# A diffusion layer with 32 experts on one core: one size of weight slot for all experts, and another order of the routing chain

## The chip, the cores and the metric

The program runs on one core of a Trainium2 chip. The metric is the device time of one execution in microseconds (us). The kernel before was run three times: 2148.13 to 2154.74 us, median 2150.1 us. The profile is of one further execution.

## The reference

One layer over 1024 tokens of width 1024. The first part mixes tokens (a state-space branch and a pooling branch, merged by gates, one output projection). A post-norm follows, and then a mixture of 32 experts in 4 groups of 8. Cut to what the change touches, with `hf` the normed and modulated tokens:

```
lg  = hf @ w_rg + b_rg                       # 4 group scores; the best group is taken
le  = (hf @ w_re + b_re)[best group]         # 8 expert scores; the best two are taken
w   = p_group * softmax(top two scores)
y   = sum over the two: w * ((silu(x @ Wg[e]) * (x @ Wu[e])) @ Wd[e])
out = layer_norm(alpha * x_mid + gate * y)
```

Wg and Wu of an expert are 1024x512, Wd is 512x1024, all float32: 6 MiB for each expert, 192 MiB in all. How many tokens an expert gets is known only when the last token has been routed.

## The kernel before, in words

The mixing takes the first 1440 us or so. Then eight tiles of 128 tokens go through the output projection, the norm and the router (the loop over `t`). In each, `choose(t)` picks group and experts on VectorE; `place(t)` finds each token's rank among the tokens of the three *fixed* experts 29, 30, 31 (32 rows each) by two matmuls with a triangular and an all-ones matrix, and adds it to `pidf`, the list of tokens of these 96 rows. `place` runs five tiles late (`LAG`), so that after the last tile five of them are left. The normed tokens `hx` go to DRAM (`h2_d`, shown as `h_d`); a gather fetches rows of it by the list `xfix` (fixed experts) or by a column of `xidx` (the others) into a tile `xe`.

After the last tile comes the dispatch chain, nearly all on VectorE: count tokens for each expert, rank the other 29 experts by load, give the fullest one 256 rows (one expert, called D here), four 192 (E), eight 128 (S), twelve 64 (two of them in one block, P) and four 32 (in one block, Q), place all tokens, and make `xidx`; `tab` is the list of experts in order of rank, from which SyncE takes the addresses of their weights. The blocks run as: fixed, D, E, Q, E, E, S, P, E, and so on. In a block, TensorE transposes gathered rows (`L1394`), multiplies by gate and up (`mm`), ScalarE and VectorE make silu and product (`eh`), TensorE transposes that and multiplies by down (`py`); the result is scattered to DRAM. Blocks of one expert (D, E, S) split weights into a rounded part and a rest (`sh` on ScalarE L1372, `sl` on VectorE L1373). Blocks of several experts (fixed, Q, P) multiply in float32, each expert with its own columns of the array, at L1411.

Weights come through a ring of 16 slots of 8 KB in each partition (`wa`, `wb`), loaded in order by SyncE (`load_w`, L1227); a slot's next load waits until its last reader is done. In `load_w` a slot holds `ne` experts with `4 // ne` steps of 128 rows each: one expert fills a slot by one DMA of 1 MiB (8 KB runs), two by two of 512 KB (4 KB runs), four by four of 256 KB (2 KB runs), and the fixed three use 6 KB of a slot by three of 256 KB. So the fixed experts' weights take 24 loads of a slot, Q's and each P's likewise 24 and 12, a single's 6. Before the end of routing, 14 slots of the fixed experts are loaded ahead (12 of their 18 MiB with the two that GpSimd issues after the first gather); SyncE then waits, in its order, for slots that TensorE must first finish reading.

Of the kernel before, what the change touches and what calls it, by code (L numbers as in the profile page):

```python
# [103 lines left out]
LAG = 5  # L104
# [37 lines left out]
def _emit(tc, nc, es, ins, out, dbg, stop):  # L142
# [815 lines left out]
    gp = rg.enter_context(pool("gp", side="right"))  # L958
    r0g = row(gp, ins["ln"][0], "r0g")
    r0b = row(gp, ins["ln"][1], "r0b")  # L960
    lgt = gp.tile([P, NT, 36], F32, name="lgt")
    G2 = row(gp, mod_d[0, 2 * D:3 * D], "G2")
    B2 = row(gp, mod_d[0, D:2 * D], "B2")
# [21 lines left out]
    ohhf = gp.tile([P, NT, 2, 4], F32R, name="ohhf")  # L985
# [8 lines left out]
    def choose(t):  # L994
# [28 lines left out]
        A = gp.tile([P, NE], F32, name="A", bufs=LAG + 1)  # L1023
# [5 lines left out]

    def place(t, A):  # L1030
        def tl(shape, name):
            return gp.tile([P] + shape, F32, name=name, bufs=2)

        T.matmul(pos[:, t], cst[:, C_SPRE], A, start=True, stop=False)
        T.matmul(pos[:, t], ones, bsum[:, t], start=False, stop=True)


        pf = pos[:, t, NE - NF:]
        okf = tl([NF], "okf")
        V.tensor_scalar(okf, pf, float(FIX_CAP), None, op0=OP.is_lt)  # L1040
        pb = tl([NF], "pb")
        V.tensor_tensor(pb, pf, ct[:, 341:341 + NF], op=OP.add)
        of = tl([2, NF], "of")
        V.tensor_tensor(of, o12[:, :, t, NE - NF:], b1_(okf, 2), op=OP.mult)
        lp = tl([2, 2, NF], "lp")
        V.tensor_tensor(lp[:, 0], of, b1_(pb, 2), op=OP.mult)
        V.tensor_tensor(lp[:, 1], of, b2(aid.rearrange("p (k t) -> p k t", k=2)[:, :, t], NF), op=OP.mult)
        lv = tl([2, 2], "lv")
        V.tensor_reduce(lv, lp, axis=AX.X, op=OP.add)
        lo = lv[:, 0]  # L1050
        V.tensor_copy(ohhf[:, t, :, 0], lv[:, 1])
        ohlf = gp.tile([P, 2, P], F32R, name="ohlf", bufs=1)
        last = V.tensor_tensor(ohlf, b1_(iop, 2), b2(lo, P), op=OP.is_equal)
        for k in range(2):
            T.matmul(pidf, ohlf[:, k], ohhf[:, t, k], start=(t + k == 0), stop=(t == NT - 1 and k == 1))
        return last

    def weights():
        S.activation(ge, ge, AF.Exp)
        pg = kept.tile([P, NT], F32, name="pg")  # L1060
        V.tensor_reduce(pg, ge, axis=AX.X, op=OP.add)
        V.reciprocal(pg, pg)
        V.tensor_sub(v12[:, 1], v12[:, 1], v12[:, 0])
# [4 lines left out]
        V.tensor_tensor(wk[:, 1], wk[:, 0], v12[:, 1], op=OP.mult)  # L1068

    with pool("o_sb") as op_:  # L1070
# [10 lines left out]
        bT2 = gp.tile([P, 4, P], F32, name="bT2")  # L1081
# [60 lines left out]
        for t in range(NT):  # L1142
# [12 lines left out]
            for n in range(2):  # L1155
                if t >= LAG and n == 0:
                    place(t - LAG, As[t - LAG])
                if t >= 2 and n == 1:
                    wout(*a, 1)
                turn(r, hT, n)  # L1160
# [18 lines left out]
            G.dma_start(h2_d[t * P:(t + 1) * P], hx)  # L1179
# [30 lines left out]
    def load_w(evs):  # L1210

        ne = len(evs)
        kc = PER // ne
        res = []
        for i0 in range(0, NSTEP, kc):
            w = wslot([ne, kc, 512])
            f = slice(i0 % PER * 512, (i0 % PER + kc) * 512)
            for i, ev in enumerate(evs):
                if isinstance(ev, int):
                    src = ins["w_e"][ev, i0 // PER, :, f]  # L1220
                else:
                    src = ins["w_e"][bass.ds(ev, 1), i0 // PER, :, f].rearrange("a p f -> p (a f)")
                dst = w[:, i].rearrange("p k f -> p (k f)")
                if ns[0] - 1 in N_GA:
                    late.append((dst, src))
                else:
                    Q.dma_start(dst, src)  # L1227
            res.append(w)
        return res, kc

    late = []
# [3 lines left out]
    gathered = []  # L1235
    loads = []

    def gather(xi):
        xe = xes[nblk[0] % NXE]
        if nblk[0] < NXE:  # L1240
            with tc.issue_after(loads[1].ins) if nblk[0] > 1 else ExitStack():
                G.memset(xe, 0.0)
        nblk[0] += 1
        ga = G.indirect_dma_start(out=xe, out_offset=None, in_=h2_d[:, :],  # L1244
                                  in_offset=bass.IndirectOffsetOnAxis(ap=xi, axis=0), bounds_check=L - 1,
                                  oob_is_err=False)
        loads.append(ga)
        return xe


    with pool("gq", side="right") as gq:
# [3 lines left out]
        def rows_of(pid, n, name, x, y=None):  # L1255

            fi = tl([n], name + "f")
            V.tensor_scalar(fi, pid, 0.0, 8192.0, op0=OP.is_equal, op1=OP.mult)
            V.tensor_tensor(fi, fi, pid, op=OP.add)
            gi = tl([n], name + "g")  # L1260
            V.tensor_scalar(gi, fi, float(L + 1), -float(L), op0=OP.is_ge, op1=OP.mult)
            V.scalar_tensor_tensor(x, gi, -1.0, fi, op0=OP.add, op1=OP.add)
            if y is not None:
                V.tensor_scalar(y, fi, -1.0, None, op0=OP.add)

        rows_of(pidf[:, 0:1], 1, "fx", xfix)
        gathered.append(gather(xfix))
        for w, src in late:
            with tc.issue_after(loads[-1].ins):
                G.dma_start(w, src)  # L1270

        e32 = slice(0, NE)
        fixed, ecol = ct[e32, 337:338], ct[e32, 340:341]
        pc = bank("st")
        cr = pc[:, 0:NE]
        cc = pc[e32, NE:NE + 1]
        T.matmul(cr, ones, bsum[:, NT], start=True, stop=True)
        T.matmul(cc, bsum[:, NT], ones[:, 0:1], start=True, stop=True)
        kr = tl([NE], "kr", NE)
        kc = tl([1], "kc", NE)  # L1280
        V.scalar_tensor_tensor(kr, cr[e32], 32.0, ct[e32, 40:72], op0=OP.mult, op1=OP.add)
        V.scalar_tensor_tensor(kc, cc, 32.0, ct[e32, 336:337], op0=OP.mult, op1=OP.add)
        V.tensor_scalar(kr, kr, kc, None, op0=OP.is_gt)
        rk = tl([1], "rk", NE)
        V.tensor_reduce(rk, kr, axis=AX.X, op=OP.add)
        V.scalar_tensor_tensor(rk, fixed, 64.0, rk, op0=OP.mult, op1=OP.add)

        ns_ = len(STEPS)
        cb2 = tl([2, ns_], "cb2", NE)
        V.tensor_scalar(cb2[:, 0], ct[e32, 144:144 + ns_], rk, None, op0=OP.is_gt)  # L1290
        V.tensor_scalar(cb2[:, 1], ct[e32, 144:144 + ns_], rk, None, op0=OP.min)
        V.tensor_tensor(cb2, cb2, ct[e32, 152:152 + 2 * ns_].rearrange("p (a n) -> p a n", a=2), op=OP.mult)
        cols = tl([3], "cols", NE)
        V.tensor_reduce(cols[:, 0:2], cb2, axis=AX.X, op=OP.add)
        V.tensor_tensor(cols[:, 0:2], cols[:, 0:2], ct[e32, 338:340], op=OP.add)
        cap = cols[:, 0:1]

        rem = tl([1], "rem", NE)
        V.tensor_tensor(rem, cc, cap, op=OP.subtract)
        nbx = tl([8], "nbx", NE)  # L1300
        V.tensor_scalar(nbx, ct[e32, 72:80], rem, None, op0=OP.is_lt)
        nb = tl([1], "nb", NE)
        V.tensor_reduce(nb, nbx, axis=AX.X, op=OP.add)
        po = pc[e32, 64:65]
        T.matmul(po, cst[e32, C_SPRE, 0:NE], nb, start=True, stop=True)
        ovs = tl([1], "ovs", NE)
        V.tensor_copy(ovs, po)
        V.tensor_scalar(cols[:, 2:3], ovs, 128.0, float(NSTAT), op0=OP.mult, op1=OP.add)
        V.tensor_tensor(cols[:, 2:3], cols[:, 2:3], cap, op=OP.subtract)
        V.tensor_tensor(cols[:, 1:2], cols[:, 1:2], cols[:, 2:3], op=OP.subtract)  # L1310
# [3 lines left out]
        T.matmul(rows, ones[e32], dg, start=True, stop=True)  # L1314
# [20 lines left out]
        for h in range(2):  # L1335
# [3 lines left out]
            for j0 in (8 * h, 8 * h + 4):  # L1339
                ohl = gq.tile([P, 4, P], F32R, name="ohl", bufs=3)  # L1340
# [305 lines left out]
```

## Time and profile before

| | us |
|---|---|
| median of three runs | 2150.1 |
| profiled execution | 2157.08 |
| its span, first to last instruction | 2155.3 |
| TensorE busy in it | 2001.2 |
| VectorE busy | 1393.1 |
| ScalarE busy | 895.3 |
| mean granted TensorE clock | 0.971 |

All rows are of one core. PE is TensorE's multiplications, PEld its loads of the stationary operand, DVE VectorE, ACT ScalarE, POOL GpSimd, SP SyncE. In a row "[0.42 <-DMA wb]" is the idle time of the engine before it and what ended that. L1343 is line 1343 of the kernel before.

### The profile page before, as it was taken

To read this page: it belongs to the slowest core of one execution; us is meant where nothing else is said; L and a number is where in the kernel's file an instruction comes from. 1 tells how busy PE (TensorE), PEld (TensorE's weight loads), DVE (VectorE), ACT (ScalarE), POOL (GpSimd) and SP (SyncE) were. 2 spreads that over 40 slices of the span, in tenths; PEclk is the share of its full clock that TensorE was granted. 3 is DMA by queue.
4 is the path that set the end of the run, shared out by engine and by line. 5 is a ranking of instruction groups with operands and counts; after the bars stand their busy time and mean duration, and the time that the engine had idled before them with its cause. 6 is when DMAs were issued, how large, how long until landed. Compare 5 with 4: busy or idle time off the path is not lost. (4 is left out here: it accounts for less than half of the span.)

```text
span 2155.3 us, 28781 instructions
## 1 busy us (share of the span) xinstructions
PE 2001.2 (93%) x10086; PEld 1521.6 (71%) x10086; DVE 1393.1 (65%) x2281; ACT 895.3 (42%) x1589; POOL 453.4 (21%) x435
## 2 busy tenths in 40 slices
PE   6998999999999999999999998989699899999985
PEld 3787788887888888888878787777365576554452
DVE  4554467779668887877665765687553576543377
ACT  3422254455454655655342331221143465533362
POOL 3233211112122222321101111253310021200003
PEclk9999999999999999999999999999699999999997
DMA  7122234333443332443477666526699999999966
GB/s 302 59 96 78 96 100 111 113 99 104 120 129 98 108 114 82 148 137 97 158 266 229 222 223 190 186 92 212 228 384 342 405 394 386 380 413 410 407 247 239
DMA packets 171902, 441.93 MB, mean 205 GB/s; under 512 B 19997, under 2 KB 54045, under 8 KB 160745
## 3 DMA queue, kind: packets, MB, share of 16 engines
q1 hardware_dynamic: 154282, 399.67, 52.8%
q0 software_dynamic: 9984, 26.75, 3.2%
q10 hardware_dynamic: 7488, 13.63, 1.7%
q8 instruction: 80, 1.31, 0.3%
q14 instruction: 68, 0.56, 0.1%
HBM read 403.01 MB, written 46.28 MB: 208 GB/s over the span
## 5 line engine op out<-in xcount | busy, mean ns | idle before, releaser
L186 PE MATMUL mm<-hh,whi 128*128 128x512 f32 x1024 | 415.1, 405 | 0.0
L188 PE MATMUL mm<-hh,wlo 128*128 128x512 f32 x1024 | 401.4, 392 | 4.2 <-DVE wlo L183 4.2
L187 PE MATMUL mm<-hl,whi 128*128 128x512 f32 x1024 | 401.1, 392 | 0.0
L188 PEld LDWEIGHTS mm<-hh,wlo 128*128 128x128 f32 x1024 | 192.9, 188 | 46.1 <-DVE wlo L183 4.6
L186 PEld LDWEIGHTS mm<-hh,whi 128*128 128x128 f32 x1024 | 193.1, 189 | 38.4 <-issue 2.6
L187 PEld LDWEIGHTS mm<-hl,whi 128*128 128x128 f32 x1024 | 193.5, 189 | 35.6 <-issue 0.2
L1372 ACT ACTIVATE sh<-wb 128x512 fp32r<-128x512 f32 x280 | 169.7, 628 | 96.0 <-DMA wb<-in_w_e_dram 22.6
L704 ACT ACTIVATE rb<-rb,tmx 128x128 f32<-128x128 f32 x512 | 163.2, 390 | 106.5 <-POOL rb L697 105.0
L1373 DVE TENSOR_TENSOR sl<-wb,sh 128x512 fp32r<-128x512 f32 x280 | 180.4, 685 | 38.9 <-ACT sh L1372 32.9
L183 DVE TENSOR_TENSOR wlo<-wraw,whi 128x1024 fp32r<-128x1024 f32 x65 | 81.7, 1257 | 161.7 <-ACT whi L182 151.4
L697 POOL TENSOR_SCALAR_AFFINE_SELECT rb<-rb 128x512 f32<-128x512 f32 x128 | 110.5, 869 | 301.9 <-DMA rb<-sr_d 229.8
L186 PE MATMUL mm<-zh,bhi 128*128 128x512 f32 x384 | 154.0, 401 | 2.2 <-ACT bhi L182 2.2
L188 PE MATMUL mm<-zh,blo 128*128 128x512 f32 x384 | 152.5, 397 | 0.4 <-DVE blo L183 0.4
L187 PE MATMUL mm<-zl,bhi 128*128 128x512 f32 x384 | 152.3, 397 | 0.0
L182 ACT ACTIVATE whi<-wraw 128x1024 fp32r<-128x1024 f32 x65 | 68.5, 1053 | 129.3 <-PE mm L187 86.4
L182 ACT ACTIVATE bhi<-braw 128x1024 fp32r<-128x1024 f32 x48 | 50.8, 1059 | 142.0 <-PE mm L187 124.5
L1411 PE MATMUL mm<-wb,xh 128*64 128x512 f32 (+1 forms) x516 | 108.9, 603 | 0.3 <-ACT xh L1400 0.3
L518 DVE SCALAR_TENSOR_TENSOR xT<-craw,sm,xT 128x1284 f32<-128x1284 f32 x64 | 101.4, 1585 | 3.1 <-ACT xT L516 2.8
L1244 POOL DMA_INDIRECT xe<-h_d,xidx x25 | 27.3, 1091 | 333.9 <-PE tr L1394 304.5
L187 PE MATMUL mm<-sl,xh 128*128 128x512 f32 x224 | 88.7, 396 | 5.1 <-DVE sl L1373 5.1
L183 DVE TENSOR_TENSOR blo<-braw,bhi 128x1024 fp32r<-128x1024 f32 x48 | 65.7, 1369 | 39.4 <-ACT bhi L182 36.9
L186 PE MATMUL mm<-sh,xh 128*128 128x512 f32 x224 | 89.0, 397 | 2.1 <-ACT sh L1372 2.1
(470 smaller groups left out, 4054.8 us busy)
## 6 DMA issues: line engine op xcount, KB each, us to landing
wb<-in_w_e_dram SPq DMA_DIRECT2D x70, 1024.0 KB
wb<-in_w_e_dram SPq DMA_DIRECT2D x120, 512.0 KB
wb<-in_w_e_dram SPq DMA_DIRECT2D x142, 256.0 KB
wraw<-in_w_blk_dram SPq DMA_DIRECT2D x64, 512.0 KB
rb<-sr_d SPq DMA_DIRECT2D x128, 256.0 KB
F<-sr_d SPq DMA_DIRECT2D x64, 256.0 KB
wmr<-in_w_ada_dram SPq DMA_DIRECT2D x64, 256.0 KB
braw<-in_wa_blk_dram SPq DMA_DIRECT2D x32, 512.0 KB
```

Source lines behind the costliest of these rows:

```text
L182: S.activation(hi, src, AF.Copy)
L183: V.tensor_sub(lo, src, hi.bitcast(F32))
L186: T.matmul(ps, lh, rh, start=start, stop=False, **kw)
L187: T.matmul(ps, lh, rl, start=False, stop=False, **kw)
L188: return T.matmul(ps, ll, rh, start=False, stop=stop, **kw)
L518: V.scalar_tensor_tensor(o, raw[:, j:j + n], smc(SM_CW + b * KCONV + j), o, op0=OP.mult, op1=OP.add)
L697: G.affine_select(rv, rv, pattern=[[0, 2], [0, 2], [sg, P]], base=0, channel_multiplier=-sg, compare_op=OP.is_ge, fill=NEG_BIG)
L704: S.activation(e, e, AF.Exp, bias=tmx[:, 0, 2 * n + ih, hd:hd + 1])
L1244: ga = G.indirect_dma_start(out=xe, out_offset=None, in_=h2_d[:, :], in_offset=bass.IndirectOffsetOnAxis(ap=xi, axis=0), bounds_check=L - ...
L1372: S.activation(hi, w, AF.Copy)
L1373: V.tensor_tensor(lo, w, hi.bitcast(F32), op=OP.subtract)
L1411: T.matmul(pss[0][i * W:(i + 1) * W], ls[0][0][:, k, i * W:(i + 1) * W], wt[:, i], start=(k == 0), stop=(k == nk - 1))
```

## The change

- Every load of expert weights becomes one DMA of 1 MiB into a slot of its own (4 steps of one expert); the products of several experts read several slots. The fixed experts take 18 loads instead of 24.
- `place` handles pairs of tiles by one set of VectorE instructions, earlier (`PLACE_AT`); three tiles, in two calls, are left after the last one.
- The last tile's `hx` is made on VectorE by two instructions of high priority from `r` before its norm, instead of on GpSimd. The two instructions on `r` with r0g, r0b come after `tab` instead of after `place`.
- The fixed rows have a tile of their own (`xe_fix`) and are gathered right when `xfix` is there; unused rows take token 0 instead of being left as a cleared tile, so that the memsets of gathered tiles go away (those of the first blocks likewise).
- `ranks` (counting, ranking, `tab`) is issued before the fixed products; the fixed gate and up products are issued before the matmuls that place all tokens (`pid`).
- The lists for the first four gathered tiles are clamped to 0, `value_load`s stand behind the loads of the block before, and the one-hot tiles `ohl` have two buffers instead of three.

The core of the diff:

```
-        ne = len(evs)
-        kc = PER // ne
-        for i0 in range(0, NSTEP, kc):
-            w = wslot([ne, kc, 512])
-            f = slice(i0 % PER * 512, (i0 % PER + kc) * 512)
-            for i, ev in enumerate(evs):
+        for i0 in range(NSTEP // PER):
+            for ev in evs:
+                w = wslot([PER, 512])
...
+    def exact_product(ps, xh, w, s0, nk, ne, W):
+        for k in range(nk):
+            wt = [a[:, (s0 + k) % PER] for a in w[(s0 + k) // PER]]
+            for i in range(ne):
+                last = T.matmul(ps[i * W:(i + 1) * W], xh[:, k, i * W:(i + 1) * W], wt[i], start=(k == 0),
+                                stop=(k == nk - 1))
+            if s0 + k in (3, 2 * KD - 1):
+                marks.append(last)
...
-LAG = 5
+PLACE_AT = {5: (0, 2), 6: (2, 4), 7: (4, 5), 8: (5, 7)}
...
+            if t == NT - 1:
+                with tc.high_priority(offset=HP):
+                    V.scalar_tensor_tensor(hx, r, ag[:, 0:1], G2, op0=OP.subtract, op1=OP.mult)
+                    V.scalar_tensor_tensor(hx, hx, rs, B2, op0=OP.mult, op1=OP.add)
...
+                place(*PLACE_AT[NT])
+                place(PLACE_AT[NT][1], NT)
+                xe_fix = op_.tile([P, D], F32, name="xe_fix", tag="wor", bufs=2)
+                pc, cols, tabbed = ranks(xe_fix)
...
-            E = G if t == NT - 1 else V
-            E.tensor_tensor(hx, r, G2, op=OP.mult)
-            E.tensor_tensor(hx, hx, B2, op=OP.add)
...
-            with tc.issue_after(fence.ins) if t == NT - 1 else ExitStack():
+            with tc.issue_after(tabbed.ins) if t == NT - 1 else ExitStack():
                 E.tensor_tensor(r, r, r0g, op=OP.mult)
                 E.tensor_tensor(r, r, r0b, op=OP.add)
...
-            with tc.issue_after(loads[1].ins) if nblk[0] > 1 else ExitStack():
-                G.memset(xe, 0.0)
...
+        for m in range(2):
+            ps = bank("mm")
+            exact_product(ps, xh, fixed_w, m * KD, KD, NF, FIX_CAP)
+            begun.append([ps])
...
+        with tc.issue_after(marks[0].ins):
+            T.matmul(rows, ones[e32], dg, start=True, stop=True)
...
+                with tc.issue_after(marks[1].ins):
+                    for j in range(4):
+                        T.matmul(pid, ohl[:, j], ohh[:, j0 + j], start=(j0 + j == 0), stop=(j0 + j == 2 * NT - 1))
...
-    weights()
-    block([(xfix, yidx[:, 0:1], False)], fixed_w, len(FIXED), FIX_CAP)
+    weights(placed)
+    block([(xfix, yidx[:, 0:1], False)], fixed_w, len(FIXED), FIX_CAP, begun)
```

The order of instructions is the same on TensorE up to the last tiles of the routing. There, TensorE's order before had the fixed products (L1411) behind the matmuls that place all tokens (L1343):

```order
L1278 MATMUL st<-cst,bsum 32x1
L1055 MATMUL mm<-ohhf,ohlf 128x4 x4
L1305 MATMUL st<-nb,cst 32x1
L1314 MATMUL st<-dg,cst 128x96
L1394 MATMUL st<-cst,xe_12416 128x128 x4
L1394 MATMUL tr<-cst,xe_12416 128x128 x4
L1343 MATMUL py<-ohh,ohl 128x50 x4
L1352 MATMUL py<-oh,rct 1x64
L1353 MATMUL py<-nb,cst 1x1
L1343 MATMUL py<-ohh,ohl 128x50 x12
L1411 MATMUL mm<-wa_12360,xh 32x512 x3
```

Now the fixed rows' transposes (L1343) and products (L1324) come first. The placing matmuls (now L1384) stand at the end of gate and up, and D's first gathered tile (`xe_12396`) is transposed ahead of the fixed experts' down product:

```order
L1324 MATMUL mm<-wb_12386,xh 32x512
L1324 MATMUL mm<-wb_12388,xh 32x512
L1324 MATMUL mm<-wb_12390,xh 32x512
L1384 MATMUL py<-ohh,ohl 128x50 x16
L1481 MATMUL tr<-cst,eh 128x96 x4
L1435 MATMUL st<-cst,xe_12396 128x128 x3
L1324 MATMUL py<-wb_12392,ehh 32x512
```

In the order before, the first transposes of D's rows stood among the fixed experts' up product.

GpSimd before, from the last tile on (`hx` and its two arithmetic instructions, then memsets, gathers and the six late loads):

```order
L1177 TENSOR_TENSOR hx<-r,G_11100 128x1024
L1178 TENSOR_TENSOR hx<-hx,B_11102 128x1024
L1179 DMA h_d<-hx 128x1024
L1184 DMA r_d<-r 128x1024
L1242 MEMSET xe_12416 128x1024
L1242 MEMSET xe_12417 128x1024
L1244 DMA xe_12416<-h_d,xfix 128x1024
L1270 DMA wb_12420<-in_w_e_dram 128x512 x3
L1270 DMA wb_12421<-in_w_e_dram 128x512 x3
L1244 DMA xe_12417<-h_d,xidx 128x1024
```

GpSimd now, over the same stretch:

```order
L1259 DMA h_d<-hx 128x1024
L1082 DMA xe_fix<-h_d,xfix 128x1024
L1269 DMA r_d<-r 128x1024
L1337 DMA wb_12400<-in_w_e_dram 128x2048
L1337 DMA wb_12401<-in_w_e_dram 128x2048
L1082 DMA xe_12396<-h_d,xidx 128x1024
L1082 DMA xe_12397<-h_d,xidx 128x1024
```

GpSimd has no arithmetic left there, and the late loads are two of 1 MiB instead of six of 256 KB.

## Rows read from the trace of the kernel before

**Rows 1.** Stretches of the span: busy us and instructions of each engine
```profile
core 0: us, PE busy (x) PEld busy (x) DVE busy (x) ACT busy (x) POOL busy (x), PEclk, DMA share, GB/s
1500.00:1540.00 40.00, 20.04 (x94) 17.34 (x92) 36.52 (x132) 5.78 (x9) 18.77 (x17) 0.56 0.52 178
...
1661.00:1690.00 29.00, 22.58 (x80) 5.88 (x80) 4.99 (x8) 4.02 (x9) 3.06 (x3) 0.99 1.00 359
...
1900.00:2060.00 160.00, 147.44 (x644) 73.47 (x640) 64.90 (x103) 60.53 (x104) 10.59 (x10) 1.00 1.02 410
2060.00:2102.00 42.00, 37.86 (x160) 28.12 (x159) 37.20 (x62) 28.86 (x48) 2.14 (x2) 1.00 0.47 193
```

**Rows 2.** Two stretches inside it, with singles' loads and with Q's
```profile
1580.00:1600.00 20.00, 19.23 (x89) 15.12 (x88) 11.73 (x18) 10.18 (x19) 0.00 (x0) 1.00 1.01 416
1645.00:1685.00 40.00, 34.65 (x194) 9.20 (x186) 3.92 (x7) 3.15 (x6) 2.98 (x3) 1.00 0.99 343
```

**Rows 3.** Waits from 1661 to 1690: total, times, longest
```profile
ACT sh L1372 <- DMA wb<-in_w_e_dram: 20.6, 2, 20.3
...
PEld py L1411 <- DMA wb<-in_w_e_dram: 15.0, 19, 2.1
```

**Rows 4.** Waits from 1690 to 2102, the longest on a transfer
```profile
PEld mm L1411 <- DMA wb<-in_w_e_dram: 1.4, 5, 0.3
```

**Rows 5.** TensorE by start and duration: fixed products, D's start, Q, the next E
```profile
1536.47 1.05 PE L1343 MATMUL py<-ohh,ohl 128*128 128x50 f32 x4 [2.53 <-DVE ohh L1338]
...
1540.48 3.64 PE L1411 MATMUL mm<-wa,xh 128*32 128x512 f32 x12
1543.90 9.81 PE L1411 MATMUL mm<-wb,xh 128*32 128x512 f32 x60
...
1557.55 2.78 PE L1411 MATMUL mm<-wb,xh 128*32 128x512 f32 x18
...
1572.41 0.50 PE L186 MATMUL mm<-sh,xh 128*128 128x512 f32 x1
...
1643.27 9.21 PE L1411 MATMUL mm<-wb,xh 128*32 128x512 f32 x83
...
1666.05 3.22 PE L1411 MATMUL py<-wb,ehh 128*32 128x512 f32 x20
...
1687.53 0.50 PE L186 MATMUL mm<-sh,xh 128*128 128x512 f32 x1 [2.08 <-ACT sh L1372]
```

**Rows 6.** GpSimd, VectorE and ScalarE at the end of routing, by start and duration
```profile
1509.77 2.33 POOL L1177 TENSOR_TENSOR hx<-r,G 128x1024 f32<-128x1024 f32 x1 [2.20 <-ACT r L1171]
```
```profile
1508.07 0.23 DVE L1024 TENSOR_SCALAR o<-rct,e2i 128x32 f32<-128x32 f32 x1
...
1509.79 2.35 DVE L1027 TENSOR_SCALAR ge<-lgt,gmax 128x4 f32<-128x4 f32 x1
...
1521.11 1.22 DVE L1182 TENSOR_TENSOR r<-r,r0g 128x1024 f32<-128x1024 f32 x1
...
1524.37 1.93 DVE L1262 SCALAR_TENSOR_TENSOR xfix<-fxg,fxf 128x1 int32<-128x1 f32 x1
```
```profile
1539.27 1.28 ACT L1440 ACT_TABLE_LOAD   x1 [4.69 <-DVE ohl L1341]
```

**Rows 7.** GpSimd's memset and gathers, and all gathers' times to landing
```profile
1524.41 1.86 POOL L1242 MEMSET xe<- 128x1024 f32 x2
1527.17 1.08 POOL L1244 DMA_INDIRECT xe<-h_d,xfix  x1 [0.90 <-POOL xe L1242]
...
1542.27 1.04 POOL L1244 DMA_INDIRECT xe<-h_d,xidx  x1 [10.71 <-DVE xidx L1262]
```
```profile
DMA to landing us min/median/max: 4.1/8.1/11.6
```

**Rows 8.** TensorE after an idle stretch in routing
```profile
1424.76 1.11 PE L1134 MATMUL py<-cst,r 128*128 128x128 f32 x4 [3.62 <-DVE r L1128]
...
1433.35 0.41 PE L188 MATMUL mm<-woh,ml 128*128 128x512 f32 x1
```

More of the change, by code (lines that the diff above doesn't have):

```diff
@@ L1028, in choose, with place @@
         return A
-    def place(t, A):
+    def place(t0, t1):
+        n = t1 - t0
         def tl(shape, name):
[L1032 to L1039, printed above, removed]
-        V.tensor_scalar(okf, pf, float(FIX_CAP), None, op0=OP.is_lt)
[L1041 to L1056, printed above, removed]
@@ L1058, in weights @@
-    def weights():
+            return gp.tile([P] + shape, F32, name=name + str(n), bufs=1)
+        for t in range(t0, t1):
+            T.matmul(pos[:, t], cst[:, C_SPRE], As[t], start=True, stop=False)
+            T.matmul(pos[:, t], ones, bsum[:, t], start=False, stop=True)
+        pf = pos[:, t0:t1, NE - NF:]
+        okf = tl([n, NF], "okf")
+        V.tensor_scalar(okf, pf, float(FIX_CAP), None, op0=OP.is_lt)
+        pb = tl([n, NF], "pb")
+        V.tensor_tensor(pb, pf, b1_(ct[:, 341:341 + NF], n), op=OP.add)
@@ new lines, in place, with weights @@
+        V.tensor_copy(ohhf[:, :, t0:t1, 0], lv[:, 1].rearrange("p (k t) -> p k t", k=2))
+        ohlf = gp.tile([P, 2 * n, P], F32R, name="ohlf", tag="bT2", bufs=1)
+        V.tensor_tensor(ohlf, b1_(iop, 2 * n), b2(lv[:, 0], P), op=OP.is_equal)
+        for t in range(t0, t1):
+            for k in range(2):
+                T.matmul(pidf, ohlf[:, k * n + t - t0], ohhf[:, k, t], start=(t + k == 0),
+                         stop=(t == NT - 1 and k == 1))
+    e32 = slice(0, NE)
+    def weights(last):
@@ L1155, in _emit @@
             for n in range(2):
-                if t >= LAG and n == 0:
-                    place(t - LAG, As[t - LAG])
+                if n == 0 and t in PLACE_AT:
+                    place(*PLACE_AT[t])
                 if t >= 2 and n == 1:
@@ L1226, in load_w @@
                 else:
[L1227 to L1231, printed above, removed]
+                    loads.append(Q.dma_start(dst, src))
+                res[-1].append(w)
+        return res
+    late, loads = [], []
     fixed_w = load_w(list(FIXED))
     nblk = [0]
[L1235 to L1240, printed above, removed]
-            with tc.issue_after(loads[1].ins) if nblk[0] > 1 else ExitStack():
-                G.memset(xe, 0.0)
[L1243 to L1248, printed above, removed]
+    def exact_product(ps, xh, w, s0, nk, ne, W):
[6 more added lines that the diff above has]
+                marks.append(last)
+    marks = []
     with pool("gq", side="right") as gq:
@@ L1266, in _emit @@
-        rows_of(pidf[:, 0:1], 1, "fx", xfix)
-        gathered.append(gather(xfix))
-        for w, src in late:
[L1269 to L1289, printed above, removed]
@@ L1309, in _emit @@
-        V.tensor_tensor(cols[:, 2:3], cols[:, 2:3], cap, op=OP.subtract)
-        V.tensor_tensor(cols[:, 1:2], cols[:, 1:2], cols[:, 2:3], op=OP.subtract)
+        for w, src in late:
+            G.dma_start(w, src)
+        xh = gq.tile([P, KD, P], F32, name="xh")
+        for kk in range(2):
+            pt = quad("mm")
+            for i in range(4):
+                T.transpose(pt[:, i], xe_fix[:, (4 * kk + i) * P:(4 * kk + i + 1) * P], ident)
+            S.activation(xh[:, 4 * kk:4 * kk + 4], pt, AF.Copy)
@@ L1385, in block @@
         xs = []
-        for xi, yi, half in idx:
-            xe = gathered.pop(0) if gathered else gather(xi)
+        for xi, yi, half in idx if begun is None else ():
+            xe = xes[nblk[0] % NXE]
+            nblk[0] += 1
+            gather(xe, xi)
             xh = ep.tile([P, KD, P], F32 if exact else F32R, name="xh", bufs=2)
@@ L1426, in folded @@
             return dst
-        pgu = []
-        for m in range(2):
+        pgu = begun or []
+        for m in range(0 if begun else 2):
             pss = [bank("mm") for _ in idx]
@@ L1469, in block @@
             scat.append(sc)
-    weights()
-    block([(xfix, yidx[:, 0:1], False)], fixed_w, len(FIXED), FIX_CAP)
+    weights(placed)
+    block([(xfix, yidx[:, 0:1], False)], fixed_w, len(FIXED), FIX_CAP, begun)
     for r, row0, n, ne, half in ORDER:
-        evs = [nc.sync.value_load(tab[0:1, r + i:r + i + 1], min_val=0, max_val=NE - 1) for i in range(ne)]
+        with tc.issue_after(loads[-1].ins):
+            evs = [nc.sync.value_load(tab[0:1, r + i:r + i + 1], min_val=0, max_val=NE - 1) for i in range(ne)]
         block([(xidx[:, b:b + 1], yidx[:, b:b + 1], half and b > row0 // P)
@@ L1493, in _emit @@
         V.tensor_tensor(dgw[:, i], b1_(ident, 2), b2(wk[:, :, t], P), op=OP.mult)
-    nov = nc.values_load(tab[0:1, 64:65], min_val=0, max_val=NOV)
+    with tc.issue_after(loads[-1].ins):
+        nov = nc.values_load(tab[0:1, 64:65], min_val=0, max_val=NOV)
     with tc.For_i(0, nov, 1) as i:
```

176 lines of the change are left out of this document (106 added, 70 removed).

## The prediction

> **What bounds the kernel now.** I read the stretches first, for the place where TensorE is not full. In [rows 1] the reader is to see three stretches. From 1500 to 1540 TensorE is busy 20.04 of 40 us at a clock of 0.56, while VectorE is busy 36.52: the routing chain on VectorE bounds. From 1661 to 1690 TensorE is busy 22.58 of 29 us, with the DMA queues full (share 1.00): the transfers bound. From 1900 to 2060 TensorE is busy 147.44 of 160 us at full clock, and the waits say the rest: from 1690 to 2102 the largest group of waits of TensorE on a transfer is 1.4 us [rows 4]. There, TensorE bounds.
>
> Then I read the waits of the second stretch [rows 3]: ScalarE waits 20.3 us in one piece for a slot of the E after Q, and TensorE's loads of Q's down product wait 15.0 us in 19 pieces. So Q and what follows stand behind the weights. The rates in [rows 2] say why: at the same share of about 1 the queues move 416 GB/s in the stretch with D's and E's 8 KB runs, and 343 GB/s in the one with Q's 2 KB runs.
>
> Last I read TensorE in order of time [rows 5]: the fixed products begin at 1540.48, end their up part at 1557.55 + 2.78 = 1560.3, and D begins at 1572.41. Q begins at 1643.27 and the next E at 1687.53.
>
> **The change, part by part.** The changed order is the same on TensorE up to the last tiles of routing, so nothing earlier should move. There are two gains to work out: the head (routing to D) and Q's stall.
>
> *Head, to xfix.* Four things go ahead of `xfix`, which ends at 1524.37 + 1.93 = 1526.3 [rows 6].
> - GpSimd's two `hx` instructions at 2.33 us; two small VectorE instructions beside them take 2.35 (a second like it follows) instead of 0.23: 2 x 2.1 = 4.2 us.
> - GpSimd's memset; `xfix` beside it takes 1.93 instead of about 0.2: 1.7 us.
> - Two `r` instructions at 1.22, now after `tab`: 2.4 us.
> - Against that, two `hx` instructions on VectorE, priced like those on `r`: -2.4. The paired places save some 20 small instructions, of which most filled gaps; I take 0.6.
>
> Sum 6.5: `xfix` at 1519.8. With the memset gone from GpSimd, the gather goes out at about 1520. The earliest landing is 4.1 us [rows 7], and at a DMA share of 0.52 [rows 1] I take that: 1524. Transposes and ScalarE's copies bring the first product to about 1526.
>
> *Head, fixed gate and up.* 96 records as before. The first 12 took 1543.90 - 1540.48 = 3.42 us, 0.285 each; the last 18 took 0.154 each [rows 5]. The 60 between took 9.7 us, so about 4 more were slow. I take 16 x 0.285 + 80 x 0.154 = 16.9: up ends at 1543, against 1560.3. The placing matmuls now stand behind it. Before, 16 of them lasted from 1536.47 to 1540.48; their one-hot tiles are ready for the first buffers, so I take 3.5: 1546.5. From their end to D's gather passed 1542.27 - 1540.48 = 1.8 us: gather at 1548.3.
>
> *Head, the new wait.* TensorE's order now has three transposes of D's first gathered tile ahead of the fixed down product. So that product, all the rest of the fixed block and everything of D are queued behind D's gather. With the median landing of 8.1 us [rows 7] it is there at 1556.4 (1552.4 with the shortest, 1559.9 with the longest). The product `eh` and its transposes are done near 1549.6, so TensorE sits idle for some 6.8 us. What follows an idle stretch is shown by [rows 8]: after 3.62 us idle TensorE ran at the lower level (1.2 GHz) from 1424.76 to 1433.35, 8.6 us. So of the down product's 48 records about 30 go at 0.285 and 18 at 0.154, 11.4 us. With three transposes ahead and the rest of D's behind (2.3 together), D starts at 1571, against 1572.4. **Gain of the head: 1.4 us**, where `xfix` alone came 6.5 earlier and gate and up 17. Ends: with the longest landing -2; with the shortest and half of the low clock about +7, and about +10 with no idle stretch that lowers the clock.
>
> *Exponentials.* Those of the router's weights now stand between the fixed block's silu and its product on ScalarE. A table load takes 1.28 us [rows 6], two more make 2.6. The idle 6.8 us hide them; without that cover they cost 2.6 of the +10.
>
> *Q's stall.* Without waits Q would take 128 records of gate and up at 9.21 / 83 = 0.111, 14.2 us; 64 of down at 3.22 / 20 = 0.161, 10.3; and some 3.5 for silu and transposes. So the E after it could start at 1643.3 + 28 = 1671.3, and it started at 1687.53. Ten of its products ran at the lower level, 2 us more. Stall 18.2.
>
> After, Q still has 24 loads in a ring of 16. But the fixed experts use 18 slots instead of 24, and 4 MiB of what SyncE had to load behind the first free slots is there before. D's, E's and Q's first 16 loads are 28 MiB; at 416 GB/s one takes 2.5 us, 70 us in all, and they may start at 1535, when the fixed gate frees slots: on time for 1642. What is left is Q's own turnover. Its down weights are loads 17 to 24, which reuse the slots of its own gate. Gate's first half is done 32 records after the start, 1641.9 + 3.6 = 1645.5; four loads of 2.5 us take till 1655.5, four more till 1665.5, and 2 us to land: 1667.5. Down needs its second half at 1641.9 + 14.2 + 2.5 + 5.2 = 1663.8. **Stall left: 4 us, gain 14.2.** Ends: 0 us where the queue runs ahead; at 343 GB/s the eight loads take 24.5 instead of 20, and with 2 to 3 us of scatters and gathers between them the stall is 11, gain 7.
>
> The Trainium skill (DMA: Bandwidth & Descriptors, Specifications) wants at least 512 B for line rate; by that 2 KB runs are at line rate already, which is the second rival below. [Rows 2] differ from it: 343 against 416 GB/s at one share. The same section puts one core's share of the memory at about 358 GB/s; by that eight loads would take 23.4 us, the stall would be 7 and the sum 12. The trace's 416 is above it and decides.
>
> *Elsewhere.* From the E after Q on, TensorE bounds, and its instructions there are the same: 0. P's loads become twice as few and longer; the only waits they could remove are those of [rows 4]. Bounds -1 and +2.
>
> **Sum.** 1.4 + 14.2 = 15.6. The profiled execution's own 2157.08 us becomes 2141.5. It lies 7 us above the median of the runs, 2150.1, and I take the saving off that: 2134.
>
> **The rivals.**
> - *The head comes free too.* D's gather lands in 4 us, or TensorE's clock does not fall. For it: the shortest landing is 4.1, and the first gather is now out of the way. Against it: the DMA queues are refilling slots just then, and the median is 8.1. Head 10, Q 15: 25, 2125. Chance 0.18.
> - *The length of a run isn't what slowed Q.* Then the queues stay at 343 GB/s, since what limits them is the turnover of slots, which now come free four at a time, by the reading of the rule above. For it: Q's stretch is the only one with these loads, so length and turnover are not separated by any row. Against it: the share is 0.99, and queues that wait for slots would be idle. Q 7, head 1.4: 8.4, 2142. Chance 0.17.
> - *The later stretch takes it back.* From 1900 to 2060 the queues are full (share 1.02, 410 GB/s); if TensorE comes 15 us early to a stretch that the loads bound, it waits there. For it: that share. Against it: TensorE hardly waits [rows 4], and from 2060 to 2102 the queues move only 193 GB/s, so the loads are done long before their use. Then no gain, 2149. Chance 0.07.
> - *Slower: D's gather behind the loads.* It goes out at 1548 among refills that started at 1535, eight of 1 MiB in flight: 8.4 MB at 410 GB/s are 20.5 us. If its rows wait for all of them, it lands after 24.6 us instead of 8.1, D starts 16.5 later, and the sum is -0.9; every further load in front costs 2.5, and from a landing of 30 us on it is slower than can be mistaken. With two or three more, 2157. Against it: no gather took over 11.6 [rows 7], with 256 KB to 1 MiB loads beside it. Chance 0.05.
>
> **How the numbers follow.** The forecast, 2134, has 0.53; its own range is 2129 to 2139 by the ends of the landing and of Q's stall. The first rival adds 2125 below and the second 2142 above. A range of 2120 to 2144 leaves out the last two rivals, 0.12, and a little of the tails. About 0.3%, 6.5 us, is what a measurement tells from no change. Faster: 0.53 + 0.18 + 0.17 = 0.88; within: 0.07; slower: 0.05.
>
> **What would show it.** Right: fixed gate and up products from 1526 to 1543, ahead of the placing matmuls; VectorE's rows of 2.3 us gone; an idle stretch of 4 to 9 us on TensorE ahead of the transposes of D's first tile, then the lower clock; D near 1571; no wait of 20 us at the E after Q, which starts near 1672; over 400 GB/s beside Q. Wrong: D before 1565 or after 1576; 350 GB/s beside Q; or a P or S period that is longer than before.

## The result, and the profile after

The changed kernel takes 2136.6 us (median of six runs, 2133.0 to 2142.2), the kernel before 2154.1 (six runs, the three of the forecast among them, 2148.1 to 2162.0): a ratio of 0.992, 95% interval 0.9897 to 0.9943. The forecast was 2134 of 2150.1, a ratio of 0.9925. So it is faster, by about 17 us, as forecast.

The two profiled executions differ by more: 2157.08 and 2133.00, 24 us. A part of that is not the change's. Routing adds the output projection's product to `r` by halves of 512 columns. These rows show the adds of the second halves of the last three tiles, the last one being the last add of routing (start and duration in us), first before, then of the change with some rows around them, then the last add alone in a second profile of the change (experiment e9):

```profile
1484.22 0.69 DVE L1128 SCALAR_TENSOR_TENSOR r<-r,mm 128x512 f32<-128x512 f32 x1 [5.79 <-PE mm L188]
...
1494.08 0.67 DVE L1128 SCALAR_TENSOR_TENSOR r<-r,mm 128x512 f32<-128x512 f32 x1
...
1504.26 0.68 DVE L1128 SCALAR_TENSOR_TENSOR r<-r,mm 128x512 f32<-128x512 f32 x1
```
```profile
1477.98 0.69 DVE L1207 SCALAR_TENSOR_TENSOR r<-r,mm 128x512 f32<-128x512 f32 x1 [6.52 <-PE mm L189]
...
1486.08 0.69 DVE L1207 SCALAR_TENSOR_TENSOR r<-r,mm 128x512 f32<-128x512 f32 x1
...
1495.74 2.35 DVE L1018 TENSOR_TENSOR lem<-lgt,msk 128x32 f32<-128x32 f32 x1
...
1498.35 2.16 DVE L1004 SCALAR_TENSOR_TENSOR e<-lem,v,rct 128x32 f32<-128x32 f32 x1
1500.44 0.67 DVE L1207 SCALAR_TENSOR_TENSOR r<-r,mm 128x512 f32<-128x512 f32 x1
...
1502.13 1.28 DVE L1253 SCALAR_TENSOR_TENSOR hx<-r,bag,G 128x1024 f32<-128x1024 f32 x1
...
1506.99 0.22 DVE L1030 TENSOR_SCALAR ge<-lgt,gmax 128x4 f32<-128x4 f32 x1
...
1514.73 0.13 DVE L1097 TENSOR_SCALAR xfix<-fxg 128x1 int32<-128x1 f32 x1
```
```profile
1509.32 0.68 DVE L1207 SCALAR_TENSOR_TENSOR r<-r,mm 128x512 f32<-128x512 f32 x1
```

The reader is to see that the last add starts up to 9 us apart in two executions of one and the same program. So stages are counted from it, below and in all experiments; "the add" is this one. "D" is D's first product, "E2" the first product of the E after Q.

| us from that add | before | changed | changed, second profile | forecast |
|---|---|---|---|---|
| `xfix` is done | 22.0 | 14.4 | 14.4 | 15.5 |
| first fixed product | 36.2 | 21.3 | 21.5 | 21.7 |
| D's gather goes out | 38.0 | 41.9 | 41.9 | 44.0 |
| D's first transposes | 49.4 | 50.8 | 50.9 | 52.1 |
| D | 68.2 | 61.8 | 61.8 | 66.7 |
| D to E2 | 115.1 | 102.1 | 102.0 | 101 |
| E2 to the end | 467.8 | 466.8 | 468.7 | unchanged |
| sum | 651.0 | 630.8 | 632.6 | 635 |

So the change took 18 to 20 us behind that row: 6 in the head, 13 from D to E2. The rest of the 24 lies ahead of it.

The row is not out of the change's reach, though. Five tiles are placed ahead of it now, and three before. The last two steps between the adds above take 9.9 + 10.2 = 20.0 us before, and as much in e1, which has the old routing chain; they take 8.1 + 14.4 = 22.5 in the changed kernel, and as much within 0.1 in all twelve profiles with the new chain. The product of the last add was done near 1496.6 on TensorE, and the add came at 1500.44, behind the two VectorE instructions of 2.35 and 2.16 us shown:

```profile
1496.23 0.39 PE L189 MATMUL mm<-woh,ml 128*128 128x512 f32 x1
```

So some 2.4 us of what is won behind the add is lost just ahead of it. Counted from the add two before, the change takes 16 to 18 us (671.1 before to the end, 653.2 and 655.0 in the two profiles), and of that 3.9 in the head; the timed runs say 17.

TensorE of the changed kernel in order of time (start, us, engine, line, tile; in brackets the idle time before and what ended it), which answers to [rows 5]:

```profile
1519.81 1.97 PE L1343 MATMUL mm<-cst,xe_fix 128*128 128x128 f32 x8 [1.92 <-DMA xe_fix<-h_d,xfix]
1521.71 1.07 PE L1324 MATMUL mm<-wa,xh 128*32 128x512 f32 x2
...
1538.13 1.07 PE L1384 MATMUL py<-ohh,ohl 128*128 128x50 f32 x8
1539.54 1.23 PE L1384 MATMUL py<-ohh,ohl 128*128 128x50 f32 x8 [0.34 <-DVE ohl L1381]
1542.77 0.81 PE L1481 MATMUL tr<-cst,eh 96*128 96x96 f32 x4 [2.01 <-DVE eh L1478]
1551.21 0.90 PE L1435 MATMUL st<-cst,xe 128*128 128x128 f32 x3 [7.62 <-DMA xe<-h_d,xidx]
1552.04 6.28 PE L1324 MATMUL py<-wb,ehh 128*32 128x512 f32 x25
...
1562.28 0.50 PE L187 MATMUL mm<-sh,xh 128*128 128x512 f32 x1 [0.25 <-ACT xh L1441]
...
1563.08 0.66 PE L1435 MATMUL st<-cst,xe 128*128 128x128 f32 x4
...
1664.42 0.50 PE L187 MATMUL mm<-sh,xh 128*128 128x512 f32 x1 [0.23 <-ACT sh L1411]
```

The fixed gate and up run ahead of the placing matmuls, the new wait is there (7.62 us on D's gather), and E2 has no wait in front of it where 20 us of waiting stood before [rows 3]. In the waits from 1640 to 1690 no product of Q waits on a transfer any more; what is left is ScalarE's, working ahead:

```profile
ACT sh L1411 <- DMA wb<-in_w_e_dram: 7.8, 2, 6.1
```

Stretches of the changed kernel (columns as in [rows 1]; the last three numbers are clock, DMA share, GB/s):

```profile
1542.00:1543.00 1.00, 0.23 (x2) 0.23 (x3) 0.77 (x4) 0.90 (x2) 0.67 (x1) 0.96 1.01 426
1543.00:1544.00 1.00, 0.58 (x4) 0.29 (x2) 0.89 (x4) 0.32 (x1) 0.70 (x2) 0.50 1.01 426
...
1553.00:1555.00 2.00, 2.00 (x12) 0.47 (x9) 0.00 (x0) 0.00 (x0) 0.00 (x0) 0.50 1.05 426
1555.00:1557.00 2.00, 2.00 (x12) 0.50 (x9) 0.00 (x0) 0.00 (x0) 0.00 (x0) 0.61 1.02 416
1557.00:1559.00 2.00, 2.00 (x18) 0.47 (x12) 0.93 (x2) 0.00 (x0) 0.00 (x0) 1.00 0.99 406
...
1620.00:1630.00 10.00, 9.65 (x47) 6.18 (x48) 6.70 (x12) 5.17 (x10) 1.32 (x1) 1.00 0.40 124
...
1650.00:1660.00 10.00, 8.53 (x58) 3.06 (x54) 2.14 (x4) 1.96 (x4) 2.04 (x2) 1.00 1.01 422
...
1900.00:2040.00 140.00, 128.53 (x567) 67.56 (x566) 61.38 (x99) 54.80 (x95) 9.61 (x9) 0.99 1.01 420
```

Three things are to be read. After the idle 7.6 us the down product starts at half clock and is at full clock from 1557 on. But the clock did not fall in that idle stretch: it was at 0.50 from 1543 on, when TensorE transposed `eh`, ahead of the wait and behind the placing matmuls and 2.01 us of idle. Beside Q the queues now move 422 GB/s where it was 343 [rows 2]. And from 1620 to 1630 they are busy only 0.40 of the time: the ring is full and SyncE waits for slots, by its waits from 1615 to 1635 for three of them whose last reader is the split of weights on VectorE. The loads have room that they did not have before.

```profile
SPq L1310 <- DVE sl L1412: 16.5, 3, 8.6
```

### The profile page after: what moved, and what is told of

The parts are those of the page before. It is cut to its first block, busy times and chain, and to the rows that moved or that the text cites. A ratio compares the mean times of both kernels' runs of the same rounds, so it can differ in the third digit from the quotient of the medians.

```text
span 2131.2 us, 28257 instructions
## 1 busy us (share of the span) xinstructions
PE 1981.6 (93%) x10086; PEld 1520.1 (71%) x10086; DVE 1393.0 (65%) x2259; ACT 897.0 (42%) x1591; POOL 437.0 (21%) x425
## 5 line engine op out<-in xcount | busy, mean ns | idle before, releaser
L1411 ACT ACTIVATE sh<-wb 128x512 fp32r<-128x512 f32 x280 | 169.0, 628 | 83.5 <-PE mm L189 20.2
L1324 PE MATMUL mm<-wb,xh 128*64 128x512 f32 (+1 forms) x560 | 116.7, 599 | 0.3 <-ACT xh L1441 0.3
L183 ACT ACTIVATE bhi<-braw 128x1024 fp32r<-128x1024 f32 x48 | 50.8, 1058 | 140.2 <-PE mm L188 132.0
```

What stands on the lines that cost most here:

```text
L183: S.activation(hi, src, AF.Copy)
L1324: last = T.matmul(ps[i * W:(i + 1) * W], xh[:, k, i * W:(i + 1) * W], wt[i], start=(k == 0), stop=(k == nk - 1))
L1411: S.activation(hi, w, AF.Copy)
```

## Experiments

All are compared with the kernel before on the same chip; stage times are from one profile each.

**e1, slots alone.** The kernel before, only with the new `load_w` and its readers.

```
-            w = wslot([ne, kc, 512])
...
+                w = wslot([PER, 512])        # one expert, 4 steps; the routing chain as before
...
```

Expected: 

> The kernel before with the full 8 KB slots alone (18 loads for the fixed experts, every load 1 MiB; routing chain and order of the products as before). My theory: the long runs and the 4 MiB ahead remove Q's stall whatever the head does; D starts where it did (1572, within 2), the E after Q about 15 us earlier than before (1673), no wait of 20 us there, over 400 GB/s beside Q. Time 13 to 15 us below before, ratio 0.993 to 0.994. Rival (Q's stall went because the head came earlier and the loads with it): the E after Q starts less than 7 us earlier, ratio 0.997 or above.

Measured: ratio 0.9917 (0.9892 to 0.9943). From the add, D at 67.0, D to E2 102.5. What Q's down product still waits (the waits from 1640 to 1690):

```profile
PEld py L1408 <- DMA wb<-in_w_e_dram: 3.0, 2, 2.7
PE py L1408 <- DMA wb<-in_w_e_dram: 1.8, 1, 1.8
```

Q's gain comes from the slots alone, without the earlier head: 12.6 of 13.0 us. The rival, that the stall went only because the head came earlier, is out. By its timed ratio this kernel can't be told from the whole change (0.992). By the profiles, from the add two before the last to the end, it takes 657.4 us against 653.2 and 655.0: the routing chain brings 2 to 4 us on top of the slots, hardly more than the last stage drifts.

**e2, routing chain alone.** The changed kernel with the slots and loads of before.

```
-                w = wslot([PER, 512])
...
+            w = wslot([ne, kc, 512])         # and f, src, dst as before
...
```

Expected: 

> The changed kernel with the slots of before (fixed, Q and P in loads of 2 KB and 4 KB runs; the routing chain, own tile and early fixed products stay). My theory, that the two parts add up: D starts near 1562 as in the changed kernel (10 us earlier than before), Q's stall stays at about 18, the E after Q starts near 1678: ratio to before 0.995. Rival (the loads are bound from their first free slot on, so that an earlier head gives the loads its 20 us too): the stall shrinks below 8 us, the E after Q starts before 1668, ratio 0.992 or below, as the full change.

Measured: ratio 0.9964 (0.9945 to 0.9983). D at 65.4: the gather lands as in the changed kernel, but TensorE's order is another behind it, as in e5 below, where the rows stand. From 1550 to 1578 the down product waits on no transfer. D to E2 108.5, between the two theories: the head gives the loads an earlier start, and that is worth 6.6 us of the 13. Waits from 1640 to 1690:

```profile
ACT sh L1414 <- DMA wb<-in_w_e_dram: 13.8, 2, 13.5
PEld py L1327 <- DMA wb<-in_w_e_dram: 7.6, 8, 2.5
```

So the parts do not add up in that stretch: 12.6 from the slots and 6.6 from the head remove the same wait, of which there are 13.0.

**e3, Q in 2 KB runs.** The changed kernel, each of Q's loads as four:

```
-                    loads.append(Q.dma_start(dst, src))
+                    for j in range(PER if len(evs) == 4 else 1):
+                        f = slice(j * 512, j * 512 + 512) if len(evs) == 4 else slice(0, SLOT)
+                        loads.append(Q.dma_start(dst[:, f], src[:, f]))
```

Expected: 

> The changed kernel with each of Q's 24 loads of 1 MiB into the same slot issued as four of 256 KB, each one step of 512 columns (2 KB runs); slots and their turnover as in the changed kernel. Run length (my theory): 340 to 350 GB/s in the stretch of Q's loads instead of 420, the E after Q starts 4 to 9 us later than in the changed kernel (1664). Turnover of slots (rival): the rate stays above 400 GB/s and E starts within 2 us of 1664.

Measured: ratio 0.9924 (0.9901 to 0.9947), not apart from the change's. D to E2 is 105.6, 3.5 later than in the change, just below what I expected from run length; and the rate, 389 at a share of 1.04, lies between the theories:

```profile
1650.00:1660.00 10.00, 8.59 (x73) 2.88 (x66) 0.69 (x1) 1.20 (x2) 0.00 (x0) 1.00 1.04 389
```

No loads of E2 lie in this stretch (every packet in it is smaller than 8 KB). So 2 KB runs bring the rate from 422 to 389, but not to the 343 of the kernel before. The slots and loads of before have 342 with the new routing chain too (e2):

```profile
1645.00:1685.00 40.00, 33.44 (x213) 9.81 (x211) 6.63 (x11) 4.78 (x9) 5.00 (x5) 1.00 0.99 342
```

There, four loads in a row bring one step each of four experts; in e3, four steps of one expert. Whether that makes the rest of the difference was not tried.

**e4, Q in quarters of the partitions.** As e3, with `f = slice(j * 32, j * 32 + 32)` over partitions, `dst[f], src[f]`.

Expected: 

> The changed kernel with each of Q's 24 loads issued as four of 256 KB again, but each 32 partitions of the full 8 KB run. If the length of the run decides (my theory), it is as the changed kernel: above 400 GB/s beside Q, the E after Q within 2 us of 1664. If the size of a transfer decides (fewer bytes under way behind the same number of transfers), it falls to 340 to 350 GB/s as the one with 2 KB runs, and E starts 4 to 9 us later.

Measured: ratio 1.0076 (1.005 to 1.0103), D to E2 137.9. Neither theory: the queues are full and move far less than with 2 KB runs.

```profile
1670.00:1680.00 10.00, 4.59 (x25) 1.38 (x26) 0.00 (x0) 0.00 (x0) 0.00 (x0) 0.54 1.00 222
```

The transfers' reach over the partitions changed with their size, so this run does not separate size from length. The Trainium skill (SBUF — State Buffer, "Door 1: The DMA port swizzle") has transfers to 32 partitions reach half of the ports, with about 218 GB/s as the limit; the trace's 222 GB/s is near it.

**e11 and e12, Q in halves.** Two transfers of 512 KB for each load over all partitions: every second step (2 KB runs) in e11, two steps in a row (4 KB runs) in e12.

```
...
+                            ks = slice(j, PER, 2)               # e11
+                            ks = slice(2 * j, 2 * j + 2)        # e12
+                            loads.append(Q.dma_start(w[:, ks], sr[:, ks]))
```

Expected (e11): 

> The changed kernel with each of Q's 24 loads issued as two of 512 KB over all 128 partitions, each every second step: 2 KB runs. Beside the next run only the length of a run differs. If run length decides: 340 to 375 GB/s at a share of 1 in the stretch of Q's loads, D to the E after Q 104 to 107 us. If the size of a transfer decides: between the 420 of 1 MiB and the 345 to 370 of 256 KB, and as the next run.

Expected (e12): 

> As the run before, but each half is two steps in a row: 4 KB runs, same size and number of transfers, same slots. If run length decides: above 390 GB/s at a share of 1, D to the E after Q 102 to 103.5 us. If size decides: as the run with 2 KB runs.

Each was run once (2144.6 and 2138.7 us), so no timed ratio is given. Measured, e11 and then e12:

```profile
1650.00:1660.00 10.00, 8.53 (x54) 2.98 (x49) 1.71 (x3) 1.58 (x3) 0.00 (x0) 1.00 1.05 389
```
```profile
1650.00:1660.00 10.00, 8.09 (x48) 2.90 (x47) 2.25 (x4) 1.58 (x3) 1.03 (x1) 1.00 1.03 410
```

GB/s over share: 370 with 2 KB runs of 512 KB, 374 with 2 KB runs of 256 KB (e3), 398 with 4 KB runs, 418 with 8 KB runs. D to E2: 105.4, 105.6, 104.2 and 102.1. So in the changed kernel's slots the length of a run sets the rate, and the size of a transfer does not between 256 and 512 KB. e11 came out as run length has it, e12 too in its rate, and 0.7 us beyond my bound in time.

**e5, the fixed experts in 24 slots again**, all else as changed (the old `load_w` for three experts).

Expected: 

> The changed kernel, only the fixed experts' weights again in 24 slots of 6 KB (three loads of 256 KB each); Q, P and the singles keep the full slots. Times are counted from the add of the last routing tile (r, first half of 512), since what comes before drifts by some us from run to run. In the changed kernel D starts 61.9 us after it and the E after Q 102.1 us after D; before, 68.1 and 115.1. If the 4 MiB ahead are a main part of Q's gain (my theory): from D to E 105 to 112 us, since 4 MiB at 420 GB/s are 10 us of loads more. If the length of Q's runs is all (rival): 102 to 104. D may come later as well, since the down weights (8 slots instead of 4) start only when the fixed products run: up to 3.5 us as in the run with all slots of before (65.3).

Measured: ratio 0.9933 (0.9909 to 0.9957), D at 64.8, D to E2 102.3. The 4 MiB that the new slots load ahead bring nothing from D to E2: the rival is right, to some 1.5 us, since D's stretch up to Q is 1.3 us shorter than in the changed kernel and Q's 1.5 longer. D starts 2.9 us later, but not for a wait on the down weights. The only such wait from 1545 to 1575 is 0.7 us; the second tile of D's rows is transposed ahead of D's first product here (in the changed kernel behind it, at 1563.08):

```profile
1568.56 0.66 PE L1457 MATMUL st<-cst,xe 128*128 128x128 f32 x4
...
1570.12 0.66 PE L1457 MATMUL tr<-cst,xe 128*128 128x128 f32 x4
...
1571.99 0.71 PE L187 MATMUL mm<-sh,xh 128*128 128x512 f32 x2
```
```profile
PEld py L1346 <- DMA wb<-in_w_e_dram: 0.7, 1, 0.7
```

**e6, the last hx on GpSimd.** The two instructions of high priority removed, and

```
-            if t < NT - 1:
-                V.tensor_tensor(hx, r, G2, op=OP.mult)
-                V.tensor_tensor(hx, hx, B2, op=OP.add)
+            E = G if t == NT - 1 else V
+            E.tensor_tensor(hx, r, G2, op=OP.mult)
+            E.tensor_tensor(hx, hx, B2, op=OP.add)
```

Expected: 

> The changed kernel with the last tile's two hx instructions back on GpSimd, behind the norm on ScalarE. My theory: small VectorE instructions beside them take 2.3 us again (two or three rows), h_d goes out 7 to 9 us later than now and the fixed gather stands behind it: first fixed product 2 to 5 us later than 21.3 us after the last tile's add, D 2 to 5 us later than 61.9. Rival (GpSimd's arithmetic lies beside a VectorE wait and costs nothing): all within 1 us.

Measured: ratio 0.9928 (0.9904 to 0.9951). First fixed product at 23.5 (2.2 later), D at 62.6 (0.7 later: the rest is lost to the gather's wait). GpSimd and VectorE, in order of time:

```profile
1516.18 2.33 POOL L1253 TENSOR_TENSOR hx<-r,G 128x1024 f32<-128x1024 f32 x1 [2.91 <-ACT r L1251]
1518.60 2.34 POOL L1254 TENSOR_TENSOR hx<-hx,B 128x1024 f32<-128x1024 f32 x1
```
```profile
1516.39 2.17 DVE L1029 TENSOR_TENSOR bsum<-bsum,A 128x32 f32<-128x32 f32 x1
...
1518.67 2.28 DVE L1004 SCALAR_TENSOR_TENSOR g<-lgt,gmax,rct 128x4 f32<-128x4 f32 x1
```

Small VectorE instructions end with GpSimd's again, as in [rows 6].

**e7, D's transposes behind the fixed down product.**

```
-            if s0 + k in (3, 2 * KD - 1):
+            if s0 + k in (3, 2 * KD - 1, NSTEP - 1):
...
-                    T.transpose(pt[:, i], xe[:, k * P:(k + 1) * P], ident)
+                    with tc.issue_after(marks[2].ins) if nblk[0] < 3 else ExitStack():
+                        T.transpose(pt[:, i], xe[:, k * P:(k + 1) * P], ident)
```

Expected: 

> The changed kernel with the transposes of D's gathered rows held behind the fixed experts' down product in TensorE's order; nothing else. My theory of the remaining head: TensorE idled 7.6 us in front of those transposes, and the lower clock after it cost some 3. So the down product runs at once after eh, no idle stretch over 3 us, D starts 6 to 9 us earlier: 53 to 56 us after the last tile's add. What comes of it at the end: if the loads have room (share 0.78 between 1572 and 1640), 5 to 9 us faster than the changed kernel, ratio to before 0.988 to 0.990; if the loads bound the stretch from D to the E after Q, D to E grows by the same amount and the time is as the changed kernel's, 0.992.

Measured: ratio 0.9917 (0.9889 to 0.9945). D at 54.0, 7.8 earlier; D to E2 unchanged at 102.1, so nothing of it is given back to the loads. The timed ratio alone could not show a gain. TensorE ahead of and in the down product:

```profile
1550.34 0.90 PE L1482 MATMUL tr<-cst,eh 96*128 96x96 f32 x4 [2.01 <-DVE eh L1479]
1551.88 6.38 PE L1324 MATMUL py<-wb,ehh 128*32 128x512 f32 x25 [0.64 <-ACT ehh L1484]
```

The wait is gone, and the low clock is not. It falls at the same place, in the 2.01 us ahead of the transposes of `eh`:

```profile
1549.00:1550.00 1.00, 0.00 (x0) 0.00 (x0) 1.00 (x9) 1.00 (x1) 0.10 (x1) 0.89 0.97 410
1550.00:1551.00 1.00, 0.66 (x4) 0.61 (x4) 0.74 (x3) 0.47 (x2) 0.94 (x1) 0.50 0.98 410
```

**e8 and e10, the placing early too.** As e7; besides, the matmul on `dg` goes out in `ranks`, and the placing matmuls behind gate (`s0 + k in (3, 7, ...)` instead of 15).

Expected (e8): 

> As the run with the transposes behind the down product, and also the matmul that spreads the capacities (rows) goes out with the ranks, not behind the third step of the fixed gate, and the placing matmuls stand after the fixed gate, not after up. My theory: D's gather goes out 6 to 9 us earlier (33 to 36 us after the last tile's add instead of 41.9) and is there before the down product ends, so D starts 51 to 54 us after the add, 0 to 3 us earlier than with the transposes alone. At the end: at most 3 us more than that run, since the loads come no earlier (they start when the fixed gate frees its slots).

Expected (e10, the same kernel again): 

> The kernel with the early placing and the transposes behind the down product again. Its profile had D 10.8 us earlier, counted from the add of the last routing tile, and nothing given back after; its ratio to before was 0.991, hardly below the change's 0.992, from runs on another chip or hour. If the stage times are the truth (my theory): ratio 8 to 10 us, 0.004 to 0.005, below the change's of this call. If something ahead of routing gives it back (rival): within 0.002 of the change's, and the start of routing (its first add) 5 us later than in the change's profile.

Measured: e8 0.9907 (0.9883 to 0.9931), e10 0.9883 (0.9864 to 0.9902). D's gather at 34.0 and 35.5, D at 51.0 and 53.0, D to E2 102.5 and 102.9. In e10:

```profile
1553.03 0.55 PE L1481 MATMUL tr<-cst,eh 96*128 96x96 f32 x4 [1.29 <-DVE eh L1478]
1554.22 4.05 PE L1327 MATMUL py<-wb,ehh 128*32 128x512 f32 x25 [0.64 <-ACT ehh L1483]
```

The same 25 records take 4.05 us at full clock, 6.38 in e7. In e10 the up product, not the placing, stands ahead of the transposes of `eh`.

**e9, the changed kernel again**, in one session with e10.

Expected: 

> The changed kernel as it is, again, to be compared with the next on the same chip. Two things: the ratio to before, 0.990 to 0.994; and in its profile the times from the add of the last routing tile: D 61 to 63 us after it and the E after Q 102 to 103 us after D, whatever the start of routing drifts to (1383 to 1393 in the profiles so far).

Measured: ratio 0.9932 (0.9905 to 0.9959), some 15 us, with the stage times of the table. The version of e10 is 0.005 below it, their intervals apart, which is 10.6 us of 2157; by the profiles it is 8 to 11 us up to E2. It beats both kernels: 2132.3 us, against 2145.3 of the change and 2157.5 before.

## Why the prediction was right, step by step

- **`xfix`: right but for a shift ahead of it.** 6.5 us forecast; 7.6 measured from the add, 5.2 with the 2.4 us by which the add itself comes later. Of its terms, the exchange of hx between GpSimd and VectorE was 4.2 - 2.4 = 1.8; e6 measures 2.1. The prediction had nothing earlier move, and took the paired places at a gain of 0.6; those 2.4 us are what it left out. From routing's first add to its last are 117.8 us before and 116.7 and 122.2 in the two profiles of the change, so the whole of routing drifts by more.
- **Fixed gate and up: right.** 14.5 earlier forecast, 14.9 measured from the add (12.5 with the 2.4).
- **The new wait: right in kind.** 6.8 us of idle forecast, 7.62 measured; D's gather landed after 8.9 us where 8.1 was taken. It went out 3.9 us later than before, for all the time won ahead of it. The low clock behind the wait, which the prediction puts down to it, did not come from it: it was there before the wait began, and it was there without the wait too (e7). Whether such a wait alone would have lowered it, no run shows.
- **Gain of the head: 1.4 forecast, 6.3 measured from the add, 3.9 with the 2.4. This term was mis-sized**, by 4.9 us behind the add. The prediction's own terms (1556.4, 11.4 and 2.3) make 1570.1 and not its 1571, which is 0.9 of it. Placing took 2.6 us and not 3.5, and the gather went out 2.1 earlier than I had it. It landed 0.8 later than taken. And from landing to D passed 11.1 us and not 14.6: I had taken 8.6 us of low clock from [rows 8], and here it was over 5 to 6 us after the first transposes. The working carried one observation of the low clock as if it were its length; the bounds beside it (-2 to +10) held what came.
- **Q's stall: gain 14.2 forecast, 13.0 measured from D to E2**, and the 2 us of low clock behind the stall, if they are counted to it, can't be read from the last stage, which drifts by that much. I left 4 us of stall in the sum; there is none. Q's own length, which I took as 28 us, is 102 - 71 = 31 without any wait on a transfer, since the transposes of E2's gathered tiles lie in it. So the stall was some 3 us smaller than the 18.2 of the sum, and what was left of it 4 us smaller; that the two nearly cancel is luck. Q's second down half comes some 3 us later than I had it, and its last loads are there; that this is why no stall was left is argued, no run shows it.
- **Why Q's stall went: half of the reasons given.** The runs: with 2 KB runs for Q alone 3.3 to 3.5 us come back (e3, e11). The 4 MiB ahead: nothing, as e5 shows with the early head. An earlier start of the loads, which I had not counted here, does 6.6 with the old slots (e2). What the slots do beyond Q's runs, 3 us between e2 and e3, I can't split: Q's and P's slots there hold several experts and those of the fixed experts 6 of 8 KB, and the same 2 KB runs move 342 GB/s in e2 where e3 has 389. Whether the 4 MiB matter without the early head (as in e1) wasn't tried.
- **Second rival (turnover, not run length): wrong.** The rate does follow the run; but run length alone does not make the old 343 GB/s, only 389 of 422 (e3). The rule named with it, of the Trainium skill (DMA: Bandwidth & Descriptors, Specifications), asks for 512 B; the trace differs: at 2, 4 and 8 KB it still shows 370, 398 and 418 GB/s.
- **First rival (the head comes free): wrong in its mechanism, the wait and the low clock were there.** What it offered was real, though: e10 takes it, by a change of order.
- **Third and fourth rival:** the stretch from 1900 on moves 420 GB/s at a share of 1.01 and costs no more than before (E2 to the end); D's gather took 8.9 us and not 25. The longest gather of the changed kernel did land later than any before, 17.3 us, but D's is the only one that TensorE waited for by the waits on `xe`. The landings (least, median, most):

```profile
DMA to landing us min/median/max: 5.8/8.8/17.3
```

## What to carry to other kernels

Work that is moved ahead of a chain is worth only as much as the next wait lets through: here 15 us won by the fixed products became 6 at D, because the order of one engine put the consumer of a gather in front of independent work; look for that, and move it. When two parts of a change remove the same wait, neither sum nor difference of their gains is the gain of both, so do each alone. And count stages from a row close ahead of them, since what is ahead of it drifts by more than the terms in question; but look whether the change reaches that row too, as here by 2.4 us.

## What the runs showed of the hardware

- A load in runs of 8, 4 and 2 KB in each of 128 partitions moved 418, 398 and 370 GB/s (rate over share); in quarters of 32 partitions with runs of 8 KB 222 at a share of 1.00. In the slots of before, loads in runs of 2 KB moved 343 and 342 at a share of 0.99 (before, e2).
- In the changed kernel and in e7 TensorE fell from its upper level (2.4 GHz) to its lower one (1.2 GHz) at the end of 2.01 us of idle, behind the placing matmuls with 0.34 us of idle among them. In e10, where the up product and then 1.29 us of idle stood at that place, it did not fall.
- The first add of the same program's routing came at 1383.8 and 1387.1 us in two profiles of the change (1386.4 before, so not behind the 1440 us of the description), and its last one at 1500.4 and 1509.3.
